# An encoder trunk in split fp32: in the channel mixers, a pair of blocks prepares its successor's first operands one product earlier, prompt products change places, and the last steps leave the fixed order

## The chip, the cores and the metric

One core of a Trainium2 chip runs the whole program. The metric is the device time of one execution in microseconds (us), the median of several runs. The engines are called PE (TensorE's matmuls), PEld (its weight loads), DVE (VectorE), ACT (ScalarE), POOL (GpSimd) and SP (SyncE, whose queue issues most loads).

## What is computed

A trunk of two layers over a prompt of 256 tokens and a sample of 1024, 1024 features wide. Layer 0 mixes tokens with a bidirectional RWKV-7 recurrence, layer 1 with 2-D neighbourhood attention; each is followed by a squared-ReLU MLP with 4096 hidden features. The part that matters here:

```python
def _sq_relu_mlp(h, w_up, w_down):
    return jnp.square(jax.nn.relu(h @ w_up)) @ w_down

def _trunk(x, p):
    for layer in range(DEPTH):
        h = _rms_norm(x, p['norm_mix_g'][layer])
        ...
        x = x + y          # y: the token mixer, which ends in a product with its w_o
        x = x + _sq_relu_mlp(_rms_norm(x, p['norm_mlp_g'][layer]), p['w_up'][layer], p['w_down'][layer])
```

## The kernel before

**Arithmetic.** Every matmul operand is split into a high part that TensorE takes exactly (`ah`, `hh`, `whi`, `dh`) and the rest (`al`, `hl`, `wlo`, `dl`); a product is three matmuls, high x high (L96), low x high (L97), high x low (L98). A split is a cast on ACT (weights L90, others L1367, features L1175) and a subtraction (weights L91, others L1368, features L1176).

**Tokens** lie in three segments: 0 is the prompt (256 columns), 1 and 2 are the halves of the sample (512 each). `x[s]` is the residual of a segment, eight tiles of 128 features; in the traces its names end in 3, 4, 5 for segments 0, 1, 2, and so do those of the norms, `ms`.

**`channel_layer` (L1275)** runs once per layer. It begins with the product with `w_o` (`dense`), first for segments 0 and 1, then for 2, whose results are added to `x` on DVE (L1342). Then come the split of the features, the sums of squares, and `scale(s)` (L1348 to L1355), which multiplies `x` by the squared norm so that one division at the end serves the whole MLP. The MLP goes over 32 blocks of 128 hidden features:

- `wup(f)` loads and splits the block's part of w_up: a load on SP into one raw buffer, the cast on ACT, the subtraction on POOL (L91).
- `up(f, s)` is 24 matmuls into a "ps" bank, relu on ACT (L1383), square on POOL (L1384), and for the prompt the split at once.
- `wraw(f, i)` loads half of the block's w_down (128 x 512, SP, L1391); `wcut` splits it (cast ACT, subtraction POOL).
- `down` (L1403) multiplies hidden blocks by w_down and adds the result to `x` on DVE (L1416). It serves blocks 0 and 1 and the last two.

Blocks 2 to 29 go in 14 pairs, with seven products in place of eight for the two sample segments. `pair_steps` makes three functions for a pair: `prep(n)` builds sums of weights on POOL (`ds`) and of hidden features on DVE (`ts`) (both L1431) and splits them; `product(n)` is 12 matmuls of 512 columns (L1476 to L1478) into the four "pc" banks and four adds to `x` on DVE (L1480); some products go on filling the banks of the one before, others open them anew. `prompt(n)` is 12 matmuls of 256 columns into "ps" banks, with two adds (L1491), for the prompt. `block_pair` (L1494) writes the order of one pair's steps, with the up-projections of the next pair (`U`) and its weights among them; `ahead[0](0)` is prep(0) of the next pair.

**What sets the order.** From the up-projection of block 2 on, everything lies in a block `tc.manual_schedule(engines=MANUAL)`: PE, DVE, ACT and POOL run in the order in which the code is written. SP's loads are placed by a scheduler, as is everything outside that block. Each engine runs its own queue in order and waits on semaphores.

**The tail** of a layer is the last pair of blocks, 30 and 31, with `down`. In layer 0 (`gnext` is set) each of the 24 tiles of `x` goes through add (DVE, L1416), times `ms` (L1418, DVE or, for odd tiles below 6, POOL), store (SP, L1419), split `ah` (ACT, L1175) and `al` (DVE, L1176), square (ACT, L1167) and sum of squares `acc` (POOL, L1168). Between the tiles stand the norms of a finished segment (`token_norms`: a copy `pq` of the sums on ACT, L1193, and small matmuls, L1196) and the first products of the attention's values (`V`, with the weights w_nv, split at L90 and L91). In layer 1 only the adds, the products with `ms` and the stores are left.

Of the kernel before, what the change touches and what calls it, by code (L numbers as in the profile page):

```python
# [51 lines left out]
class Trunk:  # L52
# [1222 lines left out]
    def channel_layer(self, layer, x_src, src, wname, dst, gnext=None, gate=False):  # L1275
# [3 lines left out]
        nc, tc, a, act = self.nc, self.tc, self.a, self.act  # L1279
        NF = 32  # L1280
        gmlp = V_GMLP + 8 * layer
        with ExitStack() as ctx:
            pool = lambda name, side="left": ctx.enter_context(tc.tile_pool(name=name, bufs=2, reuse_waits="tile", side=side))
            if gate:
                ctx.enter_context(self.clctx)
                wk, wp = self.clk, self.clw
            else:
                wk, wp = pool("clk", "right"), pool("clw", "right")
# [15 lines left out]
            def xload(s, k0, k1, m=None):  # L1304

                c0, c1 = SEGS[s]
                if m is not None:
                    nc.vector.tensor_copy(out=x[s][:, k0:k1, 0:1], in_=x[0][:, m:m + 1, 0:1].to_broadcast([P, k1 - k0, 1]))
                nc.sync.dma_start(x[s][:, k0:k1], x_src[k0:k1, :, c0:c1].rearrange("k p t -> p k t"))
# [4 lines left out]
            def dense(hi, lo, s, name=None):  # L1314
# [5 lines left out]
                             act[k][0][:, c0:c1], act[k][1][:, c0:c1], k == 0, k == KT - 1)  # L1320
                return ps

            ms = [wk.tile([P, c1 - c0], F32, name=f"ms{s}", bufs=1) for s, (c0, c1) in enumerate(SEGS)]
            todo = [*range(len(wo), 8), *range(8)]
            for seg in ((0, 1), (2,)):
                for m in range(8):
                    hi, lo = wo.pop(0)
                    if len(wo) < 1 and todo:
                        wo.append(self.wsplit(wp, a[wname][todo.pop(0)], 1024, nc.vector, tag="u", rb=1))
                    if seg == (0, 1):  # L1330
                        if m == 0:
                            xload(0, 0, 8)
                            xload(1, 0, 2)
                            xload(1, 2, 4)
                        elif m < 3:
                            xload(1, 2 * m + 2, 2 * m + 4, m - 1)
                        elif m < 7:
                            xload(2, 2 * m - 6, 2 * m - 4, m - 1)
                    for s in seg:
                        c0, c1 = SEGS[s]  # L1340
                        ps = dense(hi, lo, s)
                        nc.vector.tensor_tensor(out=x[s][:, m], in0=ps[:, :c1 - c0], in1=x[s][:, m], op=ALU.add)  # L1342
                        self.add_squares(wk, x, m, s, ms[s])
                for s in seg:
                    for k in range(KT):
                        self.split_x(x, k, s, gmlp)

            def scale(s):  # L1348
                c0, c1 = SEGS[s]
                n = c1 - c0  # L1350
                ps = pn.tile([P, 512], F32, name="nps", tag="nps")
                nc.tensor.matmul(ps[:, :n], ones, ms[s], start=True, stop=True)
                nc.vector.tensor_scalar(out=ms[s], in0=ps[:, :n], scalar1=1.0 / (KT * P), scalar2=RMS_EPS, op0=ALU.mult, op1=ALU.add)
                for m in range(8):
                    (nc.gpsimd if m % 2 else nc.vector).tensor_tensor(out=x[s][:, m], in0=x[s][:, m], in1=ms[s], op=ALU.mult)  # L1355

            def inverse(s, j):
                cs = slice(128 * j, 128 * j + 128)
                nc.vector.reciprocal(out=ms[s][:, cs], in_=ms[s][:, cs])

            def wup(f):
                wu[f] = self.wsplit(wp, a["w_up"][layer, f], 1024, nc.gpsimd, tag="u", rb=1)

            def split(src, s, pool, tags, bufs, eng):
                n = src.shape[1]
# [12 lines left out]
            def up(f, s, name=None, whole=True):  # L1378
                c0, c1 = SEGS[s]
                n = c1 - c0  # L1380
                ps = dense(*wu[f], s, name)
                r = wk.tile([P, n], F32, name="rl", tag="nt", bufs=6) if s else wh_.tile([P, n], F32, name="rl", tag="np", bufs=2)
                nc.scalar.activation(r, ps[:, :n], AF.Relu)  # L1383
                nc.gpsimd.tensor_tensor(out=r, in0=r, in1=r, op=ALU.mult)  # L1384
                hid[f, s] = r
                if whole or s == 0:
                    cut(f, s)

            def wraw(f, i):
                r = raws[f, i] = wd_.tile([P, 512], F32, name="raw", tag="dr", bufs=6)  # L1390
                nc.sync.dma_start(r, a["w_down"][layer, f, :, 512 * i:512 * i + 512])  # L1391

            def wcut(src):
                return split(src, 0, wd_, ("dh", "dl"), 4, nc.gpsimd)

            def wdown(f, load=True):
                for i in range(2):
                    if load:
                        wraw(f, i)
                    wd[f, i] = wcut(raws.pop((f, i)))  # L1400
# [93 lines left out]
            def block_pair(f2, cur, ahead):  # L1494

                (prep, product, prompt), f3, final = cur, f2 + 1, ahead is None
                U = lambda f, s: up(f, s, "ps", False)
                prep(1)
                product(0)
                prompt(0)  # L1500
                U(f2, 1)
                wraw(f3, 0)
                prep(2)
                product(1)
                U(f2, 2)
                wraw(f2, 1)
                prep(3)
                product(2)
                U(f2, 0)
                if not final:  # L1510
                    wup(f2 + 2)
                prep(4)
                product(3)
                prompt(3)
                U(f3, 1)
                wraw(f3, 1)
                prep(5)
                product(4)
                if not final:
                    U(f3, 2)  # L1520
                prep(6)
                product(5)
                prep(7)
                U(f3, 0)
                wraw(f2, 0)
                if not final:
                    wup(f3 + 2)
                product(6)
                prompt(6)
                if not final:  # L1530
                    ahead[0](0)
                prompt(7)

            wu, wd, hid, accs, raws = {}, {}, {}, {}, {}
            rest = [(s, j) for s, (c0, c1) in enumerate(SEGS) for j in range((c1 - c0) // P)]
            norms = lambda s: self.token_norms(wk, wh_, pn, accs[s], s)
            vw = []
# [2 lines left out]
                self.v_block(act, vw, self.scr["v1_d"], (wk, "nt", 512, 6), (pm, ("ps", "pc")[tb % 2], 3 + tb % 2), 0, tb, self.tn[:, 0, tb:tb + 1])  # L1540
            N = lambda s: lambda: norms(s)
            V = lambda tb: lambda: block(tb)
            wup(0)
            up(0, 0)
            scale(0)
            wdown(0)
            wup(1)
            up(1, 0)
            up(0, 1)
            up(1, 1)  # L1550
# [10 lines left out]
            with tc.manual_schedule(engines=MANUAL):  # L1561
                up(2, 1, None, False)
                wraw(3, 0)
                down([1], 1)
                wraw(2, 1)
                up(2, 2, None, False)
                wraw(3, 1)
                down([1], 2)
                wraw(2, 0)
                up(2, 0)  # L1570
                wup(4)
                down([1], 0)
                up(3, 1, None, False)
                cur = pair_steps(2, 3)
                up(3, 2, None, False)
                cur[0](0)
                up(3, 0)
                wup(5)
                for f in range(2, NF - 2, 2):
                    ahead = pair_steps(f + 2, f + 3) if f < NF - 4 else None  # L1580
                    block_pair(f + 2, cur, ahead)
                    cur = ahead
                    if rest and f > 4:
                        inverse(*rest.pop())
                wdown(NF - 2, False)
                cut(NF - 2, 1)
                wdown(NF - 1, False)
                cut(NF - 1, 1)
                cut(NF - 2, 2)
                up(NF - 1, 2, None, False)  # L1590
                cut(NF - 1, 2, True)
                down([NF - 2, NF - 1], 0)
                if gnext is None:
                    down([NF - 2, NF - 1], 1)
                    down([NF - 2, NF - 1], 2)
                else:

                    v0 = [self.wsplit(wp, a["w_nv"][0, :, 4 * j:4 * j + 4, :].rearrange("p k c -> p (k c)"), 1024, nc.gpsimd, tag="u", rb=1) for j in range(2)]
                    vw += [tuple(t[:, 256 * (k % 4):256 * (k % 4) + 256] for t in v0[k // 4]) for k in range(KT)]
                    down([NF - 2, NF - 1], 1, {6: [N(0)]})  # L1600
                    down([NF - 2, NF - 1], 2, {1: [V(0)], 3: [V(1)], 4: [N(1)], 5: [V(2)]})
                    for f in (V(3), V(4), N(2), V(5), *map(V, range(6, 10))):
                        f()
# [485 lines left out]
```

## Time and profile before

| | |
|---|---|
| runs, us | 4067.5, 4066.04, 4082.15; median 4067.5 |
| the profiled execution, us | 4086.64 |
| its span, us | 4084.8 |
| busy in the span | PE 3778.3 us, DVE 2337.9, POOL 1688.6, ACT 1686.3 |
| pairs of layer 0 | 1669.5 to 2378.0 us |
| tail of layer 0 | 2385.3 to 2478.0 us |
| pairs of layer 1 | 3342.0 to 4051.0 us |
| tail of layer 1 | 4051.0 to 4084.8 us |

The profile is of one execution, and its times count from the start of the span. A row of a timeline has start, duration, engine, line, operation, output and inputs by the program's names, and in brackets how long the engine was idle before and which instruction's end ended that. A row of waits has the engine with its waiting instruction, the instruction waited for, and the total, the count and the longest.

### The profile page before, as it was taken

To read this page: it belongs to the slowest core of one execution; us is meant where nothing else is said; L and a number is where in the kernel's file an instruction comes from. 1 tells how busy PE (TensorE), PEld (TensorE's weight loads), DVE (VectorE), ACT (ScalarE), POOL (GpSimd) and SP (SyncE) were. 2 spreads that over 40 slices of the span, in tenths; PEclk is the share of its full clock that TensorE was granted. 3 is DMA by queue.
4 is the path that set the end of the run, shared out by engine and by line. 5 is a ranking of instruction groups with operands and counts; after the bars stand their busy time and mean duration, and the time that the engine had idled before them with its cause. 6 is when DMAs were issued, how large, how long until landed. Compare 5 with 4: busy or idle time off the path is not lost.

```text
span 4084.8 us, 89789 instructions
## 1 busy us (share of the span) xinstructions
PE 3778.3 (92%) x36484; PEld 3171.2 (78%) x36484; DVE 2337.9 (57%) x4441; ACT 1686.3 (41%) x4128; POOL 1688.6 (41%) x1540
## 2 busy tenths in 40 slices
PE   8988998888888899999999969999989999999999
PEld 5765578778788778888888858887778788888887
DVE  5778743646564455666666652255563556666666
ACT  6777642555555431222222233366563222222222
POOL 4446541122222434454555441244442445555454
PEclk9988889999999899999999989999999999999999
DMA  4236565776664420111111115354555111111111
GB/s 141 70 102 227 204 215 135 159 166 157 162 151 113 142 88 29 39 42 37 37 39 37 41 43 158 103 123 93 112 137 188 42 34 42 39 42 40 37 38 62
DMA packets 460093, 394.81 MB, mean 97 GB/s; under 512 B 268480, under 2 KB 353856, under 8 KB 459680
## 3 DMA queue, kind: packets, MB, share of 16 engines
q1 hardware_dynamic: 425264, 327.73, 29.4%
q10 hardware_dynamic: 34416, 61.35, 4.1%
q8 instruction: 287, 4.70, 0.5%
q14 instruction: 126, 1.03, 0.1%
HBM read 270.50 MB, written 124.44 MB: 97 GB/s over the span
## 4 chain that ended last, share of the span: by engine, by line
PE 69%; DVE 10%; DMA 7%; ACT 6%; issue 4%; POOL 3%; SPq 1%; ACTq 0%; POOLq 0%; DVEq 0%
PE ps L96 12%; PE ps L98 12%; PE ps L97 12%; PE ps L1477 4%; PE wu L998 4%; PE ps L1476 4%; PE ps L1478 4%; DVE x L1480 2%; PE vps L513 1%; PE vps L514 1%; PE vps L515 1%; PE aps L998 1%; PE kps L998 1%; PE op L2001 1%; PE lps L998 1%
## 5 line engine op out<-in xcount | busy, mean ns | idle before, releaser
L96 PE MATMUL ps<-ah,whi 128*128 128x512 f32 (+1 forms) x2304 | 846.1, 367 | 7.9 <-ACT whi L90 7.1
L98 PE MATMUL ps<-ah,wlo 128*128 128x512 f32 (+1 forms) x2304 | 828.3, 360 | 6.2 <-POOL wlo L91 5.3
L97 PE MATMUL ps<-al,whi 128*128 128x512 f32 (+1 forms) x2304 | 830.4, 360 | 0.0
L96 PEld LDWEIGHTS ps<-ah,whi 128*128 128x128 f32 x2304 | 438.5, 190 | 82.7 <-ACT whi L90 9.7
L98 PEld LDWEIGHTS ps<-ah,wlo 128*128 128x128 f32 x2304 | 437.0, 190 | 80.2 <-POOL wlo L91 7.2
L97 PEld LDWEIGHTS ps<-al,whi 128*128 128x128 f32 x2304 | 438.7, 190 | 61.8 <-issue 0.5
L1480 DVE TENSOR_TENSOR x<-ps,x 128x512 f32<-128x512 f32 x784 | 484.9, 678 | 0.1
L1383 ACT ACTIVATE rl<-ps 128x512 f32<-128x512 f32 (+1 forms) x192 | 101.1, 526 | 863.6 <-PE ps L98 863.6
L1384 POOL TENSOR_TENSOR rl<-rl 128x512 f32<-128x512 f32 (+1 forms) x192 | 172.7, 899 | 685.2 <-ACT rl L1383 497.6
L91 POOL TENSOR_TENSOR wlo<-raw,whi 128x1024 fp32r<-128x1024 f32 (+1 forms) x114 | 235.2, 2064 | 223.0 <-ACT whi L90 211.6
L1477 PE MATMUL ps<-hlTrue,dh 128*128 128x512 f32 x784 | 311.5, 397 | 15.1 <-DVE hlTrue L1368 15.1
L1476 PE MATMUL ps<-hhTrue,dh 128*128 128x512 f32 x784 | 308.5, 394 | 7.2 <-DVE x L1480 7.2
L1478 PE MATMUL ps<-hhTrue,dl 128*128 128x512 f32 x784 | 308.1, 393 | 0.5 <-POOL dl L1368 0.5
L1368 DVE TENSOR_TENSOR hlTrue<-ts,hhTrue 128x512 fp32r<-128x512 f32 x112 | 139.3, 1244 | 217.7 <-ACT hhTrue L1367 217.7
L1368 DVE TENSOR_TENSOR hlTrue<-rl,hhTrue 128x512 fp32r<-128x512 f32 x98 | 105.5, 1080 | 265.6 <-ACT hhTrue L1367 265.3
L90 ACT CAST whi<-raw 128x1024 fp32r<-128x1024 f32 (+1 forms) x142 | 133.1, 937 | 189.2 <-PE ps L97 71.4
L1368 POOL TENSOR_TENSOR dl<-raw,dh 128x512 fp32r<-128x512 f32 x128 | 196.5, 1546 | 12.4 <-ACT dh L1367 11.0
L1368 POOL TENSOR_TENSOR dl<-ds,dh 128x512 fp32r<-128x512 f32 x112 | 169.0, 1509 | 63.4 <-ACT dh L1367 63.4
L1367 ACT CAST dh<-ds 128x512 fp32r<-128x512 f32 x112 | 69.3, 619 | 295.8 <-POOL ds L1431 295.8
L1477 PEld LDWEIGHTS ps<-hlTrue,dh 128*128 128x128 f32 x784 | 147.8, 188 | 52.1 <-DVE hlTrue L1368 23.4
L1476 PEld LDWEIGHTS ps<-hhTrue,dh 128*128 128x128 f32 x784 | 147.9, 189 | 38.6 <-issue 8.0
L1938 POOL TENSOR_TENSOR s<-s,mx 128x384 f32<-128x384 f32 (+1 forms) x150 | 109.7, 744 | 163.4 <-DVE mx L1937 106.5
(339 smaller groups left out, 10272.7 us busy)
## 6 DMA issues: line engine op xcount, KB each, us to landing
raw<-in_w_down_dram SPq DMA_DIRECT2D x128, 256.0 KB, 2.8
raw<-in_w_up_dram SPq DMA_DIRECT2D x64, 512.0 KB, 3.4
ar<-ar_d SPq DMA_DIRECT2D x80, 256.0 KB, 3.6
bk<-bk_d SPq DMA_DIRECT2D x80, 256.0 KB, 3.7
ar_d<-ar ACTq DMA_DIRECT2D x32, 512.0 KB, 3.3
bk_d<-bk ACTq DMA_DIRECT2D x32, 512.0 KB, 4.0
bs<-tab SPq DMA_DIRECT2D x128, 96.0 KB, 3.6
v_d<-vt ACTq DMA_DIRECT2D x80, 128.0 KB, 2.3
```

What stands on the lines that cost most here:

```text
L90: nc.scalar.copy(hi[:, cs], raw)
L91: lo_eng.tensor_tensor(out=lo[:, cs], in0=raw, in1=hi[:, cs].bitcast(F32), op=ALU.subtract)
L96: mm(ps, sh, mh, start=first, stop=False)
L97: mm(ps, sh, ml, start=False, stop=False)
L98: mm(ps, sl, mh, start=False, stop=last)
L998: self.nc.tensor.matmul(out, w, x, start=start, stop=stop, skip_group_check=free)
L1368: eng.tensor_tensor(out=lo, in0=src, in1=hi.bitcast(F32), op=ALU.subtract)
L1384: nc.gpsimd.tensor_tensor(out=r, in0=r, in1=r, op=ALU.mult)
L1476: mm(ch[j], hi[:, cs], hh, start=bool(new), stop=False, skip_group_check=True)
L1477: mm(ch[j], hi[:, cs], hl, start=False, stop=False, skip_group_check=True)
L1478: mm(ch[j], lo[:, cs], hh, start=False, stop=True, skip_group_check=True)
L1480: nc.vector.tensor_tensor(out=xv, in0=ch[j], in1=xv, op=ALU.add)
```

## The change

All of it is in `channel_layer`.

1. `wup` is defined ahead of the `w_o` products, and `wup(0)` is called before the last of them; `wup(1)` follows `up(0, 0)`, ahead of `scale(0)`.
2. In `block_pair`, prompt(0) and prompt(3) stand behind an up-projection of a sample segment and its w_down load, not right behind their products; prep(7) stands behind product(4), not product(5); at the end prompt(7) and then the next pair's prep(0) come before product(6), and prompt(6) is last.
3. The tail, from the weights of the last two blocks on, is in a block of its own in which only PE keeps the written order; ACT, DVE and POOL are ordered by the scheduler.

```diff
+            def wup(f):
+                wu[f] = self.wsplit(wp, a["w_up"][layer, f], 1024, nc.gpsimd, tag="u", rb=1)
...
             for seg in ((0, 1), (2,)):
                 for m in range(8):
                     hi, lo = wo.pop(0)
+                    if seg == (2,) and m == 7:
+                        wup(0)
...
                 prep(1)
                 product(0)
-                prompt(0)
                 U(f2, 1)
                 wraw(f3, 0)
+                prompt(0)
                 prep(2)
                 product(1)
...
                 prep(4)
                 product(3)
-                prompt(3)
                 U(f3, 1)
                 wraw(f3, 1)
+                prompt(3)
                 prep(5)
                 product(4)
+                prep(7)
                 if not final:
                     U(f3, 2)
                 prep(6)
                 product(5)
-                prep(7)
                 U(f3, 0)
                 wraw(f2, 0)
                 if not final:
                     wup(f3 + 2)
+                prompt(7)
+                if not final:
+                    ahead[0](0)
                 product(6)
                 prompt(6)
-                if not final:
-                    ahead[0](0)
-                prompt(7)
...
-            wup(0)
             up(0, 0)
+            wup(1)
             scale(0)
             wdown(0)
-            wup(1)
             up(1, 0)
...
                     if rest and f > 4:
                         inverse(*rest.pop())
+            with tc.manual_schedule(engines={mybir.EngineType.PE}):
                 wdown(NF - 2, False)
                 cut(NF - 2, 1)
```

The new lines shift the numbers: the adds of the products are L1484 (was L1480), those of the prompt L1495 (L1491), the subtractions of splits L1372 (L1368), the tail's adds L1420 (L1416) and its products with `ms` L1422 (L1418).

DVE's row at the end of a pair, before; `x_22224` and `x_22225` are segments 1 and 2, `x_22223` the prompt, and the first `hlTrue` is that of the next pair's prep(0).

```order
L1368 TENSOR_TENSOR hlFalse<-rl,hhFalse 128x256
L1480 TENSOR_TENSOR x_22224<-ps,x_22224 128x512 x4
L1491 TENSOR_TENSOR x_22223<-ps,x_22223 128x512 x2
L1368 TENSOR_TENSOR hlTrue<-rl,hhTrue 128x512
L1491 TENSOR_TENSOR x_22223<-ps,x_22223 128x512 x2
L1359 RECIPROCAL ms_22236<-ms_22236 128x128
L1431 TENSOR_TENSOR ts<-rl 128x512
L1368 TENSOR_TENSOR hlTrue<-ts,hhTrue 128x512
L1480 TENSOR_TENSOR x_22224<-ps,x_22224 128x512 x4
```

The same place after the change:

```order
L1372 TENSOR_TENSOR hlFalse<-rl,hhFalse 128x256
L1495 TENSOR_TENSOR x_22223<-ps,x_22223 128x512 x2
L1372 TENSOR_TENSOR hlTrue<-rl,hhTrue 128x512
L1484 TENSOR_TENSOR x_22224<-ps,x_22224 128x512 x4
L1495 TENSOR_TENSOR x_22223<-ps,x_22223 128x512 x2
L1366 RECIPROCAL ms_22236<-ms_22236 128x128
L1435 TENSOR_TENSOR ts<-rl 128x512
L1372 TENSOR_TENSOR hlTrue<-ts,hhTrue 128x512
L1484 TENSOR_TENSOR x_22224<-ps,x_22224 128x512 x4
```

The four adds of product(6) have moved from ahead of prep(0)'s subtraction to behind it, and two of the prompt's adds ahead of it.

DVE's row in the tail of layer 0 where the prompt's last tile meets segment 1's first ones, before:

```order
L1416 TENSOR_TENSOR x_22223<-ps,x_22223 128x256
L1418 TENSOR_TENSOR x_22223<-x_22223,ms_22234 128x256
L1176 SCALAR_TENSOR_TENSOR al_21968<-x_22223,vec,ah_21967 128x256
L1416 TENSOR_TENSOR x_22224<-ps,x_22224 128x512
L1418 TENSOR_TENSOR x_22224<-x_22224,ms_22235 128x512
L1176 SCALAR_TENSOR_TENSOR al_21954<-x_22224,vec,ah_21953 128x512
L1416 TENSOR_TENSOR x_22224<-ps,x_22224 128x512
L1176 SCALAR_TENSOR_TENSOR al_21956<-x_22224,vec,ah_21955 128x512
```

And after:

```order
L1422 TENSOR_TENSOR x_22223<-x_22223,ms_22234 128x256
L1420 TENSOR_TENSOR x_22224<-ps,x_22224 128x512
L1176 SCALAR_TENSOR_TENSOR al_21968<-x_22223,vec,ah_21967 128x256
L1422 TENSOR_TENSOR x_22224<-x_22224,ms_22235 128x512
L1420 TENSOR_TENSOR x_22224<-ps,x_22224 128x512 x2
L1176 SCALAR_TENSOR_TENSOR al_21954<-x_22224,vec,ah_21953 128x512
L1422 TENSOR_TENSOR x_22224<-x_22224,ms_22235 128x512
L1176 SCALAR_TENSOR_TENSOR al_21956<-x_22224,vec,ah_21955 128x512
```

Each `al` now has the adds of one to three later tiles ahead of it.

ACT's row at the same place, before; the two `whi` are the casts of w_nv, and `pq` is the copy of the prompt's sums, further on, behind segment 1's seventh tile.

```order
L1175 ACTIVATE ah_21967<-x_22223,vec 128x256
L1167 ACTIVATE sq<-x_22223 128x256
L90 CAST whi<-raw 128x1024 x2
L1175 ACTIVATE ah_21953<-x_22224,vec 128x512
L1164 ACTIVATE acc<-x_22224 128x512
L1175 ACTIVATE ah_21955<-x_22224,vec 128x512
```

And after:

```order
L1175 ACTIVATE ah_21967<-x_22223,vec 128x256
L1167 ACTIVATE sq<-x_22223 128x256
L1193 COPY pq<-acc 128x4x4x16
L1175 ACTIVATE ah_21953<-x_22224,vec 128x512
L1164 ACTIVATE acc<-x_22224 128x512
L1175 ACTIVATE ah_21955<-x_22224,vec 128x512
```

The `pq` copy has come up by 14 instructions, and the casts of w_nv have gone from here into the last pair.

More of the change, by code (lines that the diff above doesn't have):

```diff
@@ L1321, in dense @@
                 return ps
+            wu = {}
+            def wup(f):
+                wu[f] = self.wsplit(wp, a["w_up"][layer, f], 1024, nc.gpsimd, tag="u", rb=1)
             ms = [wk.tile([P, c1 - c0], F32, name=f"ms{s}", bufs=1) for s, (c0, c1) in enumerate(SEGS)]
@@ L1359, in inverse @@
                 nc.vector.reciprocal(out=ms[s][:, cs], in_=ms[s][:, cs])
-            def wup(f):
-                wu[f] = self.wsplit(wp, a["w_up"][layer, f], 1024, nc.gpsimd, tag="u", rb=1)
             def split(src, s, pool, tags, bufs, eng):
@@ L1527, in block_pair @@
                     wup(f3 + 2)
+                prompt(7)
+                if not final:
+                    ahead[0](0)
                 product(6)
                 prompt(6)
-                if not final:
-                    ahead[0](0)
-                prompt(7)
-            wu, wd, hid, accs, raws = {}, {}, {}, {}, {}
+            wd, hid, accs, raws = {}, {}, {}, {}
             rest = [(s, j) for s, (c0, c1) in enumerate(SEGS) for j in range((c1 - c0) // P)]
```

## The prediction

> **What bounds the kernel now.** I read the page's head first, then the windows of the stages that the diff touches, then the waits inside them. The profiled execution is 4086.64 us, 1.8 us of it outside its span.
>
> ```profile
> span 4084.8 us, 89789 instructions
> PE 3778.3 (92%) x36484; PEld 3171.2 (78%) x36484; DVE 2337.9 (57%) x4441; ACT 1686.3 (41%) x4128; POOL 1688.6 (41%) x1540
> ...
> 1669.50:2378.00 708.50, 695.30 (x3563) 586.36 (x3562) 436.41 (x647) 181.07 (x324) 357.71 (x260) 1.00 0.12 38
> 3342.00:4051.00 709.00, 695.94 (x3591) 588.43 (x3591) 442.02 (x654) 183.22 (x327) 361.46 (x262) 1.00 0.12 37
> 4051.00:4084.80 33.80, 29.04 (x151) 24.66 (x149) 26.48 (x40) 1.22 (x2) 11.00 (x10) 1.00 0.43 156
> ...
> 2385.30:2478.00 92.70, 50.78 (x289) 44.38 (x287) 45.00 (x78) 32.86 (x64) 38.62 (x33) 0.80 0.21 74
> ```
>
> A window row has the stretch, its length, the busy time of PE, weight load, DVE, ACT and POOL, and the granted clock. TensorE bounds the kernel, and the two runs of pairs above all: 695 of 708 us are matmuls, at full clock. The tail of layer 0 (2385 to 2478) is different: no engine is busy for more than 51 of its 92.7 us. The tail of layer 1 is TensorE again, 29 of 33.8 us. What a change can win in the pairs is the 13 us in each layer that are not matmuls; in layer 0's tail it can be more. The waits name both: first TensorE's in the pairs of layer 0, then TensorE's and DVE's in the tail, then TensorE's at the start of layer 0's stage (total, times, longest).
>
> ```profile
> PE ps L1477 <- DVE hlTrue L1368: 7.6, 13, 0.6
> PE ps L1476 <- DVE x L1480: 3.6, 1, 3.6
> PE ps L96 <- DVE x L1491: 2.1, 13, 0.2
> ...
> PE nps L1196 <- ACT pq L1193: 36.8, 2, 30.6
> ...
> DVE al L1176 <- ACT ah L1175: 36.3, 24, 7.7
> ...
> PE ps L98 <- POOL wlo L91: 3.4, 2, 2.4
> ```
>
> Thirteen times is once at each boundary between two of the 14 pairs; once is in the last pair. In the tail TensorE stands 30.6 us behind one copy of `pq`, and DVE 36.3 us behind `ah`, 24 times: an order of writing, not a lack of an engine.
>
> **The change part by part: the pair boundary.** TensorE there, layer 0, from the end of the last up-projection:
>
> ```profile
> 1719.04 0.40 PE L1476 MATMUL ps<-hhTrue,dh 128*128 128x512 f32 x1
> ...
> 1721.79 0.28 PE L96 MATMUL ps<-hhFalse,dh 128*128 128x256 f32 x1
> ...
> 1723.82 0.28 PE L98 MATMUL ps<-hhFalse,dl 128*128 128x256 f32 x1
> ...
> 1725.07 0.39 PE L1476 MATMUL ps<-hhTrue,dh 128*128 128x512 f32 x1
> 1726.05 0.51 PE L1477 MATMUL ps<-hlTrue,dh 128*128 128x512 f32 x1 [0.58 <-DVE hlTrue L1368]
> 1726.39 0.40 PE L1478 MATMUL ps<-hhTrue,dl 128*128 128x512 f32 x1
> ```
>
> Twelve matmuls of product(6) fill 1719.04 to 1721.79, so 0.23 us each; the 17 steps to 1723.82 are 0.12 each, so a prompt product of twelve is 1.43. From 1723.82 to 1725.07 are seven steps, 0.83, in 1.25: 0.42 lost on the prompt bank. From 1725.07 to 1726.39 are two, 0.46, in 1.32: 0.86 lost on `hlTrue`. Together 1.28 at each of 26 boundaries, 33 us.
>
> Call 1719.04 T. Afterwards TensorE runs prompt(7), product(6), prompt(6) and reaches the next product(0) at T + 1.43 + 2.75 + 1.43 = T + 5.61. Its operands are then made ahead, but it opens the four banks that product(6) has just filled, and the adds that empty them now stand on DVE behind `hlTrue`. When does that end? The first two rows are of this boundary, the next four of the place with the same queues, the up-projection, w_up subtraction and prep(4) in mid pair.
>
> ```profile
> 1721.78 2.41 POOL L91 TENSOR_TENSOR wlo<-raw,whi 128x1024 fp32r<-128x1024 f32 x1 [1.47 <-ACT whi L90]
> ...
> 1722.13 0.61 ACT L1367 CAST hhTrue<-rl 128x512 fp32r<-128x512 f32 x1
> ...
> 1752.49 2.39 POOL L91 TENSOR_TENSOR wlo<-raw,whi 128x1024 fp32r<-128x1024 f32 x1 [1.47 <-ACT whi L90]
> ...
> 1754.84 1.75 POOL L1368 TENSOR_TENSOR dl<-ds,dh 128x512 fp32r<-128x512 f32 x1
> ...
> 1753.48 1.95 DVE L1368 TENSOR_TENSOR hlTrue<-ts,hhTrue 128x512 fp32r<-128x512 f32 x1 [0.96 <-ACT hhTrue L1367]
> ...
> 1755.36 1.28 DVE L1480 TENSOR_TENSOR x<-ps,x 128x512 f32<-128x512 f32 x2
> ```
>
> In mid pair `hlTrue` starts during POOL's `wlo` and ends 0.55 us behind it; the first add (half of 1.28) ends 3.51 us after `wlo` began. At the boundary `hhTrue` is ready at T + 3.70, also within `wlo`, which begins at T + 2.74. So the first add ends at T + 6.25 and product(0) waits 0.64, and 0.10 for its restart (1726.05 to 1726.39 is 0.34, not 0.23 or so). I take 0.74 in place of 1.28: 0.54 x 26 = **-14 us**. Bounds: all 1.28 goes (-33), or POOL's `dl` gets ahead of `hlTrue` (+20, worked out with the rivals); the mid-pair row decides, since it is this very queue.
>
> **Prompt products and prep(7)** inside the pair. Two prompt products move behind up-projections: 1.43 us of cover is taken from between product(0) and U(f2,1), product(3) and U(f3,1), where no wait shows, and given to products 1 and 4. Prep(7)'s cast and subtraction come earlier on ACT and POOL; POOL has 350 us free of the 708, and its reader, prompt(7), is an up-projection away. Neither passes a DMA on SP: the w_down loads keep their places between the projections. I cost them at nothing; without that cover a POOL subtraction of 1.3 us in each pair would be 1.3 x 28 = 36 us.
>
> **The last pair** has the one wait of 3.6 us, since no up-projection stands between products 4 and 5. First and thirteenth matmul from product(5), in layer 0, then 1:
>
> ```profile
> 2365.11 0.76 PE L1476 MATMUL ps<-hhTrue,dh 128*128 128x512 f32 x1 [3.58 <-DVE x L1480]
> ...
> 2370.36 0.42 PE L96 MATMUL ps<-ah,whi 128*128 128x256 f32 x1
> ...
> 4035.05 0.47 PE L1476 MATMUL ps<-hhTrue,dh 128*128 128x512 f32 x1 [3.62 <-DVE x L1480]
> ...
> 4037.89 0.28 PE L96 MATMUL ps<-ah,whi 128*128 128x256 f32 x1
> ```
>
> Prompt(3) now runs between U(f3,1), from which DVE's late adds count, and product(4): the wait falls by 1.43 to 2.2 in each layer, -2.9. In layer 0 the product behind the wait took 5.25 us, in layer 1 2.84: it ran at half pace after 3.58 us idle, and not after 3.62. I count half of the 2.4 as won, -1.2. Together **-4** (0 to -7, if the waits go on to shrink with their adds). The Trainium skill ("TensorE: Matmul & The Clock Gate", Part 1: The HAM clock gate) has the clock halve after an idle window of some 3.4 us whose start runs free; by it 2.2 us of idling never halve it and the whole 2.4 is won, 1.2 more, and the two rows agree with a window whose phase is chance.
>
> **The start of each stage.** The first w_up block is split before the last w_o product, not behind it, and the second before the scaling. TensorE waits for `wlo` twice, 3.4 us in all. I take the longer wait, 2.4, as gone in each of two layers: **-4.8**, between 0 (the casts still queue behind ACT's `ah`) and -6.8.
>
> **The tail of layer 0.** Its orders on ACT, DVE and POOL are now the scheduler's: `al` no longer holds up the next adds, the `pq` copy stands behind its own segment, and the second w_nv cast, which had to wait for its load, comes into the last pair. What is left is what cannot overlap. The rows above have `hlTrue` take 1.95 us beside POOL; alone, DVE operations of this size take 0.7. So DVE's operations on two SBUF tiles and POOL's take turns, and DVE's adds from PSUM fit beside POOL. The groups of this window (count, busy, mean ns, idle before), then one undisturbed row of each DVE kind, then the late cast:
>
> ```profile
> L1168 POOL TENSOR_TENSOR acc<-acc,sq 128x512 f32<-128x512 f32 x14 | 17.9, 1280 | 28.3 <-ACT sq L1167 28.3
> L1176 DVE SCALAR_TENSOR_TENSOR al<-x,vec,ah 128x512 fp32r<-128x512 f32 x16 | 13.6, 849 | 28.9 <-ACT ah L1175 28.9
> L1418 DVE TENSOR_TENSOR x<-x,ms 128x512 f32<-128x512 f32 x10 | 9.5, 951 | 0.3
> L1418 POOL TENSOR_TENSOR x<-x,ms 128x512 f32<-128x512 f32 x6 | 7.6, 1272 | 8.4 <-DVE x L1416 8.4
> L1168 POOL TENSOR_TENSOR acc<-acc,sq 128x256 f32<-128x256 f32 x7 | 5.1, 732 | 8.0 <-ACT sq L1167 8.0
> L1176 DVE SCALAR_TENSOR_TENSOR al<-x,vec,ah 128x256 fp32r<-128x256 f32 x8 | 3.9, 484 | 7.5 <-ACT ah L1175 7.5
> L1418 DVE TENSOR_TENSOR x<-x,ms 128x256 f32<-128x256 f32 x5 | 2.7, 535 | 0.2
> L1418 POOL TENSOR_TENSOR x<-x,ms 128x256 f32<-128x256 f32 x3 | 2.2, 735 | 3.6 <-DVE x L1416 3.6
> ...
> 2471.49 0.69 DVE L1418 TENSOR_TENSOR x<-x,ms 128x512 f32<-128x512 f32 x1
> ...
> 2476.24 0.75 DVE L1176 SCALAR_TENSOR_TENSOR al<-x,vec,ah 128x512 fp32r<-128x512 f32 x1 [0.80 <-ACT ah L1175]
> ...
> 2412.58 1.04 ACT L90 CAST whi<-raw 128x1024 fp32r<-128x1024 f32 x1 [6.54 <-DMA raw<-in_w_nv_dram]
> ```
>
> POOL: 17.9 + 7.6 + 5.1 + 2.2 = 32.8. DVE undisturbed: 16 x 0.75 + 3.9 + 10 x 0.69 + 2.7 = 25.5. In turns 58.3, and some 3 before the first add: a floor of 61.4, 31 us under 92.7. The least that goes is the 7.7 us hole behind the late cast and a little of its wake, 9. I take **-25**, nearer the floor, since 36.3 us of DVE's time here are waits that the new order removes at their cause; the 6 us above the floor are the first and last tiles' round trips over ACT and the two norms. The w_nv casts and subtractions inside the last pair can delay a `relu` by their 1.0 us; that lies in the bounds. Layer 1's tail is TensorE's: nothing.
>
> Sum: -14 - 4 - 4.8 - 25 = -48: 4038.6 for the profiled execution. The median of the runs shown is 4067.5, 19 us below the profiled one; the terms are absolute, so I carry them over: **4019.5 us**.
>
> **The rivals.**
>
> 1. The tail gives only its hole (-9): the scheduler's order meets new round trips, or the attention stage behind it hands the gain back. For: POOL and DVE alternate, so a bad order costs turns. Against: the tail waits have one pattern, and the order breaks it. -32, 4035.5.
> 2. The boundary wait goes whole: for, if `wlo` is done sooner, all operands lie ready; against, the mid-pair rows. 19 more, 4000.5.
> 3. The boundary keeps 1.28, the new wait on the adds for the old: 4033.5. With rival 1 together 4049.5.
> 4. POOL's `dl`, 1.28 like the other POOL operations of this size, gets in before `hlTrue`: 0.74 + 1.28 = 2.02 for 1.28, +20 in place of -14: 4053.5.
> 5. Slower: POOL, whose queue is never empty there, keeps DVE out through `dl` and the sum `ds` of prep(1) behind it:
>
> ```profile
> 1725.41 1.74 POOL L1431 TENSOR_TENSOR ds<-raw 128x512 f32<-128x512 f32 x1
> ```
>
> Then product(0) waits 2.02 + 1.74 = 3.76, 2.48 more than now, x 26 = +65 against the other terms' -34: +31, 4098.5. It decides from a wait of 3.4 at each boundary. Against 4 and 5: at 1754.88 the subtraction ended, and `hlTrue`, waiting longer, went first. The Trainium skill ("SBUF — State Buffer", Who interferes with whom) says that a DVE operation with two SBUF inputs and a POOL one that reads SBUF block each other wholly, and that issue order decides; by that rule, the trace agreeing with its 1.95 against 0.7, `hlTrue` comes first and both rivals are out.
>
> **How the numbers follow.** Chances: forecast 0.48; rivals 1 and 3 0.30 (each alone 0.13 and 0.12, together 0.05); rival 2 0.14; rival 4 0.05; rival 5 0.03. A measurement of this kernel can tell about 0.5% from no change, 20 us: faster is below 4047.2, slower above 4087.8. Faster 0.48 + 0.25 + 0.14 = 0.87; same 0.05 + 0.05 = 0.10; slower 0.03. The range takes in rival 2 with the tail at its floor (4000.5 - 6 and the start's 2 more, near 3990) and rivals 1 and 3 together, 4050.
>
> **What would show it.** Right: in the pairs `hlTrue` leaves TensorE's waits and 26 waits on `x` L1484 of about 0.6 come; the wait of 3.6 falls to about 2.2; the 30.6 behind `pq` goes and layer 0's tail is near 68 us. Wrong: those waits at 2 us or absent, a tail above 80, or matmuls of the pairs taking longer in sum.

## The result, and the profile after

The changed kernel takes 4036.48 us (median of five runs, 4028.49 to 4045.69) where the kernel before takes 4069.95. The ratio is 0.9913, with a 95% interval of 0.989 to 0.9937: 35 us faster, 26 to 45. Forecast were 48 us, with 4019.5 us and a range of 3990 to 4050.

The head of the page of after, then the windows of layer 0's pairs and of its tail (columns as before):

```profile
span 4026.7 us, 89828 instructions
PE 3754.7 (93%) x36484; PEld 3158.2 (78%) x36484; DVE 2394.2 (59%) x4441; ACT 1686.2 (42%) x4128; POOL 1697.3 (42%) x1540
...
1653.00:2357.00 704.00, 693.20 (x3588) 587.15 (x3587) 465.06 (x656) 184.72 (x328) 364.55 (x263) 1.00 0.12 39
2358.00:2423.00 65.00, 51.48 (x304) 44.66 (x303) 55.63 (x79) 32.53 (x65) 43.85 (x34) 0.91 0.29 100
```

The two spans differ by 58 us, more than the runs do. The reason is in code that the change does not touch. The load of the first w_up block, here with the last w_o subtraction ahead of it on DVE, is issued 15.1 us earlier in the trace of after, before any saving could have reached it. First before, then after:

```profile
1513.37 1.23 DVE L91 TENSOR_TENSOR wlo<-raw,whi 128x1024 fp32r<-128x1024 f32 x1 [4.09 <-ACT whi L90]
...
1514.62 17.77 SPq L89 DMA_DIRECT2D raw<-in_w_up_dram  x3
```

```profile
1498.30 1.23 DVE L91 TENSOR_TENSOR wlo<-raw,whi 128x1024 fp32r<-128x1024 f32 x1 [4.10 <-ACT whi L90]
...
1499.56 16.89 SPq L89 DMA_DIRECT2D raw<-in_w_up_dram  x3
```

So one subtracts stage from stage, never span from span. Taken between the same matmuls, after gains some 42 us on before from the last w_o products on. Of these some 3 lie in the attention stage and at the starts of the two channel stages; the traces of kernels without that part of the change differ there by as much.

**The pairs.** TensorE's only wait in layer 0's pairs, thirteen at the boundaries and the one of the last pair:

```profile
PE ps L1480 <- DVE x L1484: 10.8, 14, 2.2
```

The wait on `hlTrue` (7.6) and that on the prompt bank (2.1) are gone, and a wait on the adds of product(6) stands in their place; the last pair's wait has fallen from 3.6 to 2.2. One boundary, TensorE first, then POOL, then DVE:

```profile
1702.71 0.28 PE L96 MATMUL ps<-hhFalse,dh 128*128 128x256 f32 x1
...
1708.21 0.28 PE L98 MATMUL ps<-hhFalse,dl 128*128 128x256 f32 x1
1709.15 0.47 PE L1480 MATMUL ps<-hhTrue,dh 128*128 128x512 f32 x1 [0.66 <-DVE x L1484]
1709.46 0.40 PE L1481 MATMUL ps<-hlTrue,dh 128*128 128x512 f32 x1
...
1705.45 2.40 POOL L91 TENSOR_TENSOR wlo<-raw,whi 128x1024 fp32r<-128x1024 f32 x1 [1.47 <-ACT whi L90]
1707.82 1.73 POOL L1372 TENSOR_TENSOR dl<-raw,dh 128x512 fp32r<-128x512 f32 x1
...
1706.45 1.96 DVE L1372 TENSOR_TENSOR hlTrue<-rl,hhTrue 128x512 fp32r<-128x512 f32 x1 [0.36 <-ACT hhTrue L1371]
1708.33 2.47 DVE L1484 TENSOR_TENSOR x<-ps,x 128x512 f32<-128x512 f32 x4
```

`hlTrue` starts within POOL's `wlo`, takes 1.96 us where one undisturbed takes 0.7, and the four adds follow. From 1708.21 to 1709.15 lie 0.94 us where 0.12 is the step; with the slow second step that is 0.90 lost where it was 1.28. The period of a pair falls from 54.46 to 54.10 in layer 0 and from 54.25 to 53.94 in layer 1.

The last pair differs by layer. In layer 0 the matmuls behind its wait keep their pace, where before they ran at half pace; in layer 1 it is the other way round. Layer 1, the wait and the first slow matmul, then the window from there:

```profile
3976.20 0.47 PE L1480 MATMUL ps<-hhTrue,dh 128*128 128x512 f32 x1 [2.20 <-DVE x L1484]
...
3977.80 0.63 PE L1480 MATMUL ps<-hhTrue,dh 128*128 128x512 f32 x1
...
3977.50:3980.80 3.30, 3.30 (x11) 2.63 (x10) 2.61 (x5) 1.21 (x3) 2.09 (x2) 0.50 0.00 0
```

A matmul of 512 columns takes 0.63 us there in place of 0.40, at a granted clock of 0.50, and the 1.4 us that the shorter wait had won in this layer are lost again.

**The tail of layer 0.** TensorE's waits from the first add on (with the start of the attention stage), then DVE's wait on `ah`, then DVE's first add and its last `al`:

```profile
PE vps L513 <- ACT vt L519: 7.5, 2, 6.0
PE nps L1196 <- POOL acc L1168: 6.7, 2, 6.3
PE ps L96 <- DVE x L1420: 6.2, 3, 5.5
...
DVE al L1176 <- ACT ah L1175: 5.5, 5, 2.6
...
2360.80 0.42 DVE L1420 TENSOR_TENSOR x<-ps,x 128x256 f32<-128x256 f32 x1 [3.21 <-PE ps L98]
...
2417.95 2.42 DVE L1176 SCALAR_TENSOR_TENSOR al<-x,vec,ah 128x512 fp32r<-128x512 f32 x2
```

DVE's wait on `ah` has fallen from 36.3 us to 5.5, and the 30.6 behind `pq` are gone. The chain from first add to last `al` is 2420.37 - 2360.80 = 59.6 us; before it was 88.6 (2388.38 to 2476.99). Within it DVE's idle time has fallen from 44 us to 6, but its busy time has risen from 44 to 54, since its operations now run beside POOL's. The first row shows part of what is given back: the attention stage's first products wait 7.5 us for the last values, 3.4 before. From a matmul of the last up-projections to one well inside the attention stage the trace has 149.98 us, 175.54 before: 25.6 us are left of the 29.

**The start** has gained nothing: TensorE waits for `wlo` there 5.0 us in all in layer 0, 3.4 before (layer 1: 4.2, and 1.9 before).

```profile
PE ps L98 <- POOL wlo L91: 5.0, 2, 3.7
```

### The profile page after: what moved, and what is told of

Same layout as the page of the kernel before. It is cut to its first block, busy times and chain, and to the rows that moved or that the text cites. A ratio compares the mean times of both kernels' runs of the same rounds, so it can differ in the third digit from the quotient of the medians.

```text
span 4026.7 us, 89828 instructions
## 1 busy us (share of the span) xinstructions
PE 3754.7 (93%) x36484; PEld 3158.2 (78%) x36484; DVE 2394.2 (59%) x4441; ACT 1686.2 (42%) x4128; POOL 1697.3 (42%) x1540
## 3 DMA queue, kind: packets, MB, share of 16 engines
q1 hardware_dynamic: 425264, 327.73, 29.5%
## 4 chain that ended last, share of the span: by engine, by line
PE 67%; DVE 8%; ACT 7%; issue 6%; DMA 5%; POOL 5%; SPq 1%; ACTq 0%; POOLq 0%; DVEq 0%
PE ps L96 12%; PE ps L97 11%; PE ps L98 11%; PE wu L998 4%; PE ps L1480 4%; PE ps L1482 3%; PE ps L1481 3%; POOL rl L1388 1%; PE vps L513 1%; ACT whi L90 1%; PE aps L998 1%; POOL dl L1372 1%; PE vps L514 1%; PE vps L515 1%; PE op L2005 1%
## 5 line engine op out<-in xcount | busy, mean ns | idle before, releaser
L1484 DVE TENSOR_TENSOR x<-ps,x 128x512 f32<-128x512 f32 x784 | 484.9, 678 | 0.0
L1480 PE MATMUL ps<-hhTrue,dh 128*128 128x512 f32 x784 | 309.6, 395 | 21.8 <-DVE x L1484 21.8
L1372 DVE TENSOR_TENSOR hlTrue<-rl,hhTrue 128x512 fp32r<-128x512 f32 x98 | 122.1, 1247 | 202.6 <-ACT hhTrue L1371 202.3
L1372 POOL TENSOR_TENSOR dl<-raw,dh 128x512 fp32r<-128x512 f32 x128 | 221.0, 1729 | 11.0 <-ACT dh L1371 7.0
L1372 DVE TENSOR_TENSOR hlTrue<-ts,hhTrue 128x512 fp32r<-128x512 f32 x112 | 131.2, 1171 | 150.3 <-ACT hhTrue L1371 150.3
L1480 PEld LDWEIGHTS ps<-hhTrue,dh 128*128 128x128 f32 x784 | 147.8, 188 | 53.9 <-issue 27.1
L1495 DVE TENSOR_TENSOR x<-ps,x 128x512 f32<-128x512 f32 x224 | 148.7, 685 | 68.0 <-PE ps L98 66.7
L1372 POOL TENSOR_TENSOR dl<-ds,dh 128x512 fp32r<-128x512 f32 x112 | 157.3, 1405 | 63.5 <-ACT dh L1371 63.5
```

Of the source, the lines that this page charges most:

```text
L1372: eng.tensor_tensor(out=lo, in0=src, in1=hi.bitcast(F32), op=ALU.subtract)
L1480: mm(ch[j], hi[:, cs], hh, start=bool(new), stop=False, skip_group_check=True)
L1484: nc.vector.tensor_tensor(out=xv, in0=ch[j], in1=xv, op=ALU.add)
```

## The experiments

My theory after the result: the tail's order gave most, the pairs some 15 us, the start nothing; the boundary is now bound by `hlTrue` behind POOL's `wlo`; the tail by DVE and POOL taking turns.

**One part alone.** Three kernels, each the kernel before with one part of the diff: (1) the order of `block_pair`, (2) the tail's block, (3) the place of `wup(0)` and `wup(1)`.

```diff
 (2)
                         inverse(*rest.pop())
+            with tc.manual_schedule(engines={mybir.EngineType.PE}):
                 wdown(NF - 2, False)
```

> The kernel before with the new order of block_pair alone. My theory from the two profiles: at each of 26 boundaries the wait on hlTrue (1.28 us lost) is replaced by a wait on the adds (0.9 lost), and the wait in the last pair falls by 1.4 (layer 0 more, where the half clock goes too). That gives about 0.35 x 26 + 4.2 + 1.8 = 15 us: 4055 against a kernel before of 4070. Period of a pair 54.1 in layer 0 and 53.9 in layer 1. Rival: the parts gain only together (the tail's order needs the last pair's new end); then the periods fall all the same, but the last pair and the tail of layer 0 are as before, 9 us in all.

> The kernel before with the tail alone taken out of the fixed orders. My theory: the tail's chain from the first add to the last al of layer 0 falls from 88.6 to about 60 us, some 4.6 of it is given back at the start of the attention stage, layer 1's tail does not move: 26 us faster, 4044. Rival: the chain shortens, but the gain is taken back at the start of the attention stage in a larger part (its first loads and the norm of segment 2 come last): 10 us or less.

> The kernel before with the earlier w_up split alone. By the profile of after, the load of the first w_up block cannot start earlier, since it needs the one raw buffer that the last w_o block still holds until its subtraction is done; TensorE's waits for wlo then stay (1.4 + 3.7 us where they were 1.0 + 2.4), and the time is that of before within its uncertainty, 0 us. Rival, the step of my prediction: 2.4 us in each layer, 5 us faster.

Each ratio is to the kernel before, run in the same series, with its 95% interval; 0.001 is 4 us. Measured: pairs alone 0.9975 (0.9962 to 0.9988), 10 us; tail alone 0.993 (0.9913 to 0.9947), 28 us; start alone 1.0004 (0.9992 to 1.0017), nothing. The product of the three is 0.9909 where the whole change has 0.9913: the parts add up within the intervals. In the traces the pairs alone have the periods 54.1 and 53.9 and the last pair's wait of 2.2; the tail alone has the old waits in the pairs and a tail like that of after. For the tail and the start my theories held; for the pairs the 15 us lie at the edge of what the runs allow (5 to 15), and the trace of that kernel has them. The start's rival, which was the step of the prediction, has no support: the runs allow at most 3 us of its 5.

**What bounds the boundary.** The changed kernel with the second w_up split behind prep(0):

```diff
                 wraw(f2, 0)
-                if not final:
-                    wup(f3 + 2)
                 prompt(7)
                 if not final:
                     ahead[0](0)
+                    wup(f3 + 2)
                 product(6)
```

> The changed kernel with the second w_up split of each pair placed behind prep(0) of the next pair, so that POOL's 2.4 us subtraction of 128x1024 no longer stands ahead of dl, nor ACT's cast ahead of dh and hhTrue. My theory: hlTrue is no longer held by that subtraction, ends about 1.5 us earlier or more, and the wait on the adds at the boundary (0.66, 0.9 lost) goes: the period falls from 54.1 to 53.2, 26 x 0.9 = 23 us under the changed kernel. Rival A: the adds are late because DVE gets to them late anyway (the prompt's adds and dl's hold on hlTrue): the period stays at 54.1 or falls by 0.3 at most. Rival B: the subtraction, now behind prep(0), delays prep(1)'s sum and the wait reappears as one on prep(1)'s operands at product(1).

Measured: 4012.52 us, 0.9863 (0.9845 to 0.9882), 20 us under the changed kernel's ratio. The periods are 53.17 and 53.02. Its boundary, POOL, DVE, then product(0) on TensorE, then TensorE's waits in layer 0's pairs:

```profile
1709.74 1.31 POOL L1372 TENSOR_TENSOR dl<-raw,dh 128x512 fp32r<-128x512 f32 x1 [1.04 <-PE ps L1482]
1711.22 2.65 POOL L91 TENSOR_TENSOR wlo<-raw,whi 128x1024 fp32r<-128x1024 f32 x1 [0.17 <-ACT whi L90]
...
1710.71 0.88 DVE L1372 TENSOR_TENSOR hlTrue<-rl,hhTrue 128x512 fp32r<-128x512 f32 x1
1711.52 2.47 DVE L1484 TENSOR_TENSOR x<-ps,x 128x512 f32<-128x512 f32 x4
...
1713.05 0.40 PE L1480 MATMUL ps<-hhTrue,dh 128*128 128x512 f32 x1
...
PE ps L1480 <- DVE x L1484: 2.2, 1, 2.2
```

The adds now begin 1.5 us before product(0) wants its bank, and only the last pair's wait is left. That is 0.93 in each pair, as expected; rivals A and B fall. The subtraction behind prep(0) delays nobody. The edit also takes ACT's cast of the block away from ahead of `hhTrue`, so `hlTrue` starts 0.5 us earlier; that alone would hardly have helped, as in the changed kernel it would still have started within `wlo`. The rest is its duration, 0.88 us where it was 1.96.

**What prep(0) ahead is worth, and what the prompts' places are.** Two kernels, each the changed one with one move of `block_pair` undone:

```diff
 (prep back)
                 prompt(7)
-                if not final:
-                    ahead[0](0)
                 product(6)
                 prompt(6)
+                if not final:
+                    ahead[0](0)
```

> The changed kernel with prep(0) of the next pair back behind prompt(6), so that on DVE the adds of product(6) and of prompt(6) come ahead of hlTrue. My theory: product(0) finds its banks empty, but hlTrue ends only at about 7.1 us after the last up-projection (adds to 6.4, then its own 0.7), 1.3 after TensorE wants it: 1.4 to 1.5 us lost at each boundary in place of 0.9, the period is 54.6 to 54.7, longer than the 54.46 of before, and the time 14 us above the changed kernel. Rival: prep(0) ahead is not what gained; the place of prompt(7) is; then the period stays at 54.1 or below.

> The changed kernel with prompt(0) and prompt(3) back behind their products. My theory: the steady pairs do not need them elsewhere, the period stays at 54.1 and 53.9; only the last pair loses its 1.4 us of cover, its wait goes from 2.2 to 3.6 in each layer: 3 us slower than the changed kernel, or 5 with the half clock in layer 0. Rival: their cover is what lets the operands of products 1 and 4 be ready; then a new wait comes in every pair and the period rises by up to 1.4.

Prep back: 4098.6 us, 1.0068 (1.0046 to 1.0091), 63 us above the changed kernel and slower than before too. The theory had the sign, and the size is more than four times its 14. TensorE's wait there, then POOL, DVE and TensorE at one boundary, then the window right behind its wait:

```profile
PE ps L1481 <- DVE hlTrue L1372: 28.7, 13, 2.2
...
1710.47 1.29 POOL L1372 TENSOR_TENSOR dl<-raw,dh 128x512 fp32r<-128x512 f32 x1
1711.71 1.27 POOL L1435 TENSOR_TENSOR ds<-raw 128x512 f32<-128x512 f32 x1
...
1711.04 1.28 DVE L1495 TENSOR_TENSOR x<-ps,x 128x512 f32<-128x512 f32 x2
1712.23 1.30 DVE L1372 TENSOR_TENSOR hlTrue<-rl,hhTrue 128x512 fp32r<-128x512 f32 x1
...
1713.59 0.50 PE L1481 MATMUL ps<-hlTrue,dh 128*128 128x512 f32 x1 [2.22 <-DVE hlTrue L1372]
...
1716.04 0.63 PE L1480 MATMUL ps<-hhTrue,dh 128*128 128x512 f32 x1
...
1713.60:1717.80 4.20, 4.20 (x13) 3.33 (x14) 3.45 (x6) 0.66 (x2) 1.57 (x1) 0.66 0.00 0
```

Two things were missing in the sum. `hlTrue` came to its turn at 1712.23, when `ds` of prep(1) had begun at 1711.71, so it ended only at 1713.53: this is the mechanism of the prediction's fifth rival, which needs `hlTrue` to come late. And the 2.22 us of idling are enough, at about every other boundary, for matmuls at half pace (0.63 us long, granted clock 0.66): the period is 55.66 or 57.2.

Prompts back: 4036.71 us, 0.9923 (0.9895 to 0.995), the changed kernel's within the intervals. The periods are 54.07 and 53.87, and TensorE's waits in layer 0 are the thirteen of about 0.66 with a last pair of 4.0 in place of 2.2:

```profile
PE ps L1480 <- DVE x L1484: 12.6, 14, 4.0
```

So spreading the prompts does nothing for the steady pairs and shortens the last pair, as expected.

**The start.** The changed kernel with the first w_up block's raw values in two w_down buffers, free at that time:

```diff
             def wup(f):
-                wu[f] = self.wsplit(wp, a["w_up"][layer, f], 1024, nc.gpsimd, tag="u", rb=1)
+                if f:
+                    wu[f] = self.wsplit(wp, a["w_up"][layer, f], 1024, nc.gpsimd, tag="u", rb=1)
+                    return
...
+                for c in (0, 512):
+                    raw = wd_.tile([P, 512], F32, name="raw", tag="dr", bufs=6)
+                    nc.sync.dma_start(raw, a["w_up"][layer, f, :, c:c + 512])
```

> The changed kernel with the raw values of the first w_up block loaded into two free buffers of w_down's raw halves, in place of the one raw buffer that the last w_o block holds. My theory (the one raw buffer is what kept the start from gaining): the first cast and subtraction come about 2.8 us earlier, and, the one buffer being free at 1499.5, the second block's too; TensorE's waits for wlo at the start (1.4 + 3.7) fall to 1 us or less: 4 us in each layer, 8 in all, 4026 beside a changed kernel of 4034. Rival: the casts on ACT still queue behind the splits of segment 2, or the subtraction on POOL takes turns with DVE's al: the waits stay at 3 us or more and the time moves by 2 us or less.

Measured: 4016.39 us, 0.9884 (0.9862 to 0.9906), 12 us under the changed kernel's ratio. From a fixed matmul of the last w_o products to one of the early up-projections, the trace has 50.9 us where after has 58.0 (layer 1: 53.0 and 59.9): 14 us in both layers. TensorE's waits at the start of layer 0, the whole list, ACT's first two casts, and the window from 1503 to 1531 us; behind it the same window of after:

```profile
PE ps L96 <- DVE x L1430: 0.9, 1, 0.9
...
1498.58 1.14 ACT L1334 CAST whi<-raw 128x512 fp32r<-128x512 f32 x2 [0.59 <-PE ps L97]
...
1503.00:1531.00 28.00, 27.89 (x150) 23.42 (x148) 21.14 (x22) 9.31 (x17) 18.46 (x16) 1.00 0.09 29
```

```profile
1503.00:1531.00 28.00, 22.77 (x111) 18.73 (x110) 14.73 (x17) 9.09 (x15) 13.06 (x11) 0.94 0.12 38
```

The waits for `wlo` are gone, and TensorE is busy throughout. The intervals of the two ratios overlap, so the 12 us rest on the traces as much as on the runs. The cast starts at 1498.58, some 4 us earlier than in after, released by TensorE, which frees the buffer it writes. The raw buffer was the cause: the edit also cuts the block in halves, but both halves are subtracted by 1501.82, where in after the whole block was at 1506.54. The size was more than expected: in after, the matmuls behind the wait of 3.7 us run at half pace for a while (the granted clock of the window is 0.94), and that goes with the wait.

**The tail.** Four kernels. (a) and (b) are the kernel before, all orders fixed, with the w_nv splits earlier: (a) ahead of the tail's first `down`, (b) one within the last of the 14 pairs, one behind the last up-projection. (c) is the changed kernel with all products with `ms` on DVE, (d) that with the sums of squares on DVE too.

```diff
 (c)
-    (nc.gpsimd if m % 2 and m < 6 else nc.vector).tensor_tensor(out=xv, in0=xv, in1=ms[s], op=ALU.mult)
+    nc.vector.tensor_tensor(out=xv, in0=xv, in1=ms[s], op=ALU.mult)
 (d), as well, in the tail
-    nc.gpsimd.tensor_tensor(out=acc[:, :n], in0=acc[:, :n], in1=sq[:, :n], op=ALU.add)
+    nc.vector.tensor_tensor(out=acc[:, :n], in0=acc[:, :n], in1=sq[:, :n], op=ALU.add)
```

> The kernel before with nothing changed but the place of the two w_nv splits: ahead of the last pair's first down instead of behind it; the orders stay fixed. My theory: this takes away the 7.7 us hole behind the late cast and its wake, 9 us of layer 0's tail (88.6 to 80), and no more; the other 20 us of the tail's gain come from al no longer holding up the adds behind it. Rival: the late cast is the cause of most of the tail's gain, since the copy pq and segment 1's squares queue behind it on ACT: 20 us or more.

> The kernel before, fixed orders kept, with the first w_nv split inside the last pair (where a further w_up block would be split) and the second behind the last up-projection, so that neither load is waited for; in the sixth run the wait for the load had only moved to the front of the tail (9.3 us). My theory: the hole of 7.7 us goes without a new one, the tail of layer 0 is 8 to 9 us shorter than before, and the remaining 20 us of the tail's gain belong to al's place behind the adds. Rival: the tail does not get shorter, since TensorE's next wait (the norm behind segment 1's seventh tile) takes the time back; then all of the tail's gain belongs to the order.

(a) took 1.0016 (0.9999 to 1.0032) and tells nothing of the cause: its second cast, in a fixed order, still waits for its load, now at the front, where TensorE stands 9.3 us. (b) took 0.999 (0.9976 to 1.0004). Its chain from first add to last `al` is 2456.81 - 2375.37 = 81.4 us, 7.2 under before. TensorE's waits on the adds in (a), the 9.3 us among them, then in (b) its longest waits and DVE's in the chain, and last one of DVE's waits in the kernel before:

```profile
PE ps L96 <- DVE x L1416: 13.2, 5, 9.3
```

```profile
PE nps L1196 <- ACT pq L1193: 28.6, 2, 22.1
...
DVE al L1176 <- ACT ah L1175: 29.5, 24, 2.6
```

```profile
DVE x L1416 <- PE ps L98: 2.9, 3, 1.3
```

In (b) the wait behind `pq` has lost the 8 us of the hole, and 22 stay. So by the traces 7 of the tail's 29 us were the late load, and the other 22 are the order; the runs of (b) show 4 us (-2 to 10), which agrees. Which part of the order it was, no run separates, but the waits speak for `al` and not for `pq`: DVE still stands 29.5 us behind `ah` in (b), once at each of 24 tiles, and in the kernel before its adds stood behind TensorE for 2.9 us only, while TensorE waited 30.6 for `pq`.

> The changed kernel with all products of x with ms in the tail on DVE, where nine of 24 were on POOL. My theory (DVE's operations on two SBUF tiles and POOL's take turns, and that sum is the tail's floor): POOL gives up 7.6 + 2.2 = 9.8 us, DVE takes 6 x 0.69 + 3 x 0.42 = 5.4, the sum falls from 58.3 to 53.9 and the chain from 59.6 to about 55: 4 us faster than the changed kernel in that stage. Rival: DVE and POOL do not exclude each other, and the busier of the two bounds the tail; then DVE's additional 5.4 us make it longer by up to 5 us.

> The changed kernel with the products with ms and the sums of squares of the tail all on DVE: POOL has nothing to do in the tail of layer 0. DVE alone then needs 13.9 (adds) + 15.9 (al) + 14.4 (products with ms) + 14 x 0.69 + 7 x 0.42 = 12.6 (sums), 57 us, and 2 for small operations. My theory, after the seventh run: a POOL operation on SBUF stops DVE for about as long as it runs, unless DVE is at an add from PSUM, so what POOL does there is hardly done beside DVE; without POOL the chain is as long as with it, 59 us (57 to 61). Rival: POOL works beside DVE, and the seventh run's missing gain came from the round trips over ACT; then the 12.6 us that move to DVE come on top of 59.5: 68 to 72 us.

(c) took 0.9899 (0.988 to 0.9919), within the intervals of the changed kernel, and its chain is 59.5 us like that of after: the 4 us of my theory did not come. (d) took 0.9884 (0.986 to 0.9907), and its chain is 2412.00 - 2359.00 = 53.0 us; 4.9 us of the 6.6 under after are left well inside the attention stage. By the runs alone (d) and the changed kernel are not clear of each other. The groups of DVE in (c), then in (d) (count, busy, mean ns):

```profile
L1176 DVE SCALAR_TENSOR_TENSOR al<-x,vec,ah 128x512 fp32r<-128x512 f32 x16 | 16.7, 1044 | 0.6 <-ACT ah L1175 0.6
L1422 DVE TENSOR_TENSOR x<-x,ms 128x512 f32<-128x512 f32 x16 | 14.9, 951 | 0.0
```

```profile
L1176 DVE SCALAR_TENSOR_TENSOR al<-x,vec,ah 128x512 fp32r<-128x512 f32 x16 | 11.9, 743 | 0.0
L1422 DVE TENSOR_TENSOR x<-x,ms 128x512 f32<-128x512 f32 x16 | 10.6, 683 | 0.0
L1168 DVE TENSOR_TENSOR acc<-acc,sq 128x512 f32<-128x512 f32 x14 | 9.5, 682 | 0.0
```

In both DVE has next to no idle time within the chain (0.7 and 0.1 us). With POOL out of the way each DVE operation on two SBUF tiles takes its 0.68 or 0.74 us; with POOL's sums running it takes 0.3 more. DVE does all the work, 12.4 us of it new, in 6.5 us less. The rival of (d), 68 to 72 us, is out. My own theory (59 us, as long as with POOL) missed as well: POOL does not merely fail to help here, it costs more than it carries.

**Both mends together.**

> The changed kernel with the late w_up split of the fourth run and the raw buffers of the fifth. My theory: both gains add up, 24 and 8 us under the changed kernel, 4003. If the fifth run's theory is wrong, 4011 as in the fourth.

Measured: 3991.15 us, 0.9817 (0.9791 to 0.9843), the fastest kernel run: 39 us under the changed kernel's ratio, the sum of 20 and 12 within the intervals, and clear of the fourth run's. The tail of (d) on top of it was not run.

## Why the prediction was right, point by point

- **The boundary (-14).** The mechanism came as worked out: the wait goes from `hlTrue` to the adds, 0.66 us where 0.64 was forecast, because `hlTrue` stands behind `wlo`: the fourth run removed that one cause and the wait with it. The term was too large by the restart: 0.10 was counted for TensorE's start after the wait, and 0.24 came (0.90 lost in all, not 0.74). With 0.36 and 0.31 at each of 13 boundaries, it is about -9.
- **Prompt products and prep(7) (nothing).** No new wait came in the pairs. Prompts back shows this for the prompts; prep(7) was not run alone.
- **The last pair (-4).** The wait fell by 1.4 in each layer as counted (prompts back shows the cause). Layer 0 did not run at half pace this time and won 4.6 in all; layer 1 now did, and kept 0.3 of its 1.4. That is about -5, and near the forecast by chance: which last pair runs slow changed from run to run. The sentence on the Trainium skill ("TensorE: Matmul & The Clock Gate", Part 1: The HAM clock gate) had it that 2.2 us of idling never halve the clock. In layer 0 of after they did not, but in layer 1 they did, and in the run with prep(0) back 2.22 us did at 14 of 26 boundaries. Page and measurement differ there, and the measurement decides.
- **The start (-4.8).** This step failed. It let the casts come earlier and named ACT's queue as the doubt; the load itself could not start, as its one raw buffer was held by the last w_o block to the end of its subtraction at 1499.53. Calling a load earlier moves nothing while its buffer is taken. The run of this part alone measured no gain. The size was off too: 2.4 was layer 0's longest wait for `wlo`, and layer 1's was 1.0.
- **The tail of layer 0 (-25).** The waits that it named went, and that is the mechanism. The chain went from 88.6 to 59.6, nearly to what I called the floor (58.3), 4 us more than forecast; and the attention stage took back 3 to 4 us, which the sum had at nothing and only the first rival named: -25.6 in the traces, 28 in the run of the part alone. That it comes so close to -25 is luck, two misses that cancel. The floor itself was misread, too: (c) lowered that sum by 4.4 and the chain did not follow, and the run without POOL went 5.3 under 58.3.
- **Sum.** -9 - 5 - 0 - 25.6 = -40 by the traces, and -35 (26 to 45) by the runs, for -48. The forecast's 13 us in each layer that are not matmuls are no bound on what the pairs can win: between the same matmuls layer 0's pairs became 9.3 us shorter, while TensorE's idle time there fell from 13.2 to 10.8, since the rows of matmuls overlap (0.40 us long, 0.23 apart) and hide part of a loss. Of the rivals, the second (no wait at the boundary) is what the fourth run built; the fourth and fifth did not occur, as `hlTrue` was ready before `wlo` ended, but the fifth's mechanism does when it comes later, as with prep(0) back.

## What to carry to other kernels

Before moving an operand ahead of a product, ask which engine's in-order queue it joins: here making `hlTrue` early put the adds that free the banks behind it, and 0.90 of the 1.28 us at stake hung on a subtraction of another engine. A load called earlier gains only if its buffer is free earlier. And where DVE's time in a stage is longer per operation than elsewhere, count what POOL does there: work moved from POOL to a full DVE made this stage shorter.

## What the runs showed of the hardware that I had not expected

- TensorE idle for 2.22 us came back at full pace at some boundaries and, a few matmuls later, at half pace (0.63 us a matmul for 0.39, granted clock 0.66 over 4.2 us) at others, mostly in turn. The same holds for 2.20 us in the last pair of after: full pace in layer 0, half pace in layer 1. Idle for 3.62 us in layer 1 of the kernel before it was not slowed.
- A wait of 0.66 us for another engine costs TensorE 0.90 us of its steady pace.
- POOL's running sums lengthen DVE's operations on two SBUF tiles by some 40% (683 to 951 ns, 743 to 1044 ns on average), and not its adds from PSUM (681 and 678 ns).
